# One layer of a hybrid decoder on one core: the first segment's output projection over all its tokens at once

## The chip, the core and the metric

The kernel runs on one core of one Trainium2 chip. The metric is the device time of one execution, in microseconds, as a median over runs. TensorE is written PE in the profile (PEld is its loading of stationary operands), VectorE is DVE, ScalarE ACT, GpSimd POOL and SyncE SP; SP issues nearly all DMAs here.

## What is computed

One layer over 2048 prompt tokens and 8 sample tokens, model width 1024, all in float32:

```python
h = _rmsnorm(x, norm_pre_mix)
(gq, gk, gv, gz, gb, ga, mq, mk, mv, mo, mi, mf) = _split(h @ w_in, IN_SPLITS)
...                                   # four heads of gated DeltaNet, four of mLSTM, by chunks
o = jnp.concatenate([o_gdn.reshape(Bsz, T, GDN_WIDTH), h_ml.reshape(Bsz, T, ML_WIDTH)], axis=-1)
mix = o.astype(h.dtype) @ w_out       # the output projection, 1024 x 1024
x = x + _rmsnorm(mix, norm_post_mix)
u = jnp.square(jax.nn.relu(_rmsnorm(x, norm_pre_mlp) @ w_up))
x = x + _rmsnorm(u @ w_down, norm_post_mlp)
```

## The kernel before

The prompt is cut into four segments of 512 tokens; the 8 sample tokens ride with the second one. Per segment there are stage A (input projection `w_a`, `a_units`), the recurrent mixer (`mixer`: two halves of gated DeltaNet, then four mLSTM chunks of 128 tokens, `ml_chunk`), stage B (output projection `w_o`, `b_units`), `norm_mid`, and the MLP (`cd_units`).

**A product.** Activations lie transposed, model width on partitions and tokens in columns. Every float32 operand is split into a rounded part and a rest, hi and lo, and three matmuls stand for one: hi by hi (L195), hi weights by lo activations (L196), lo weights by hi activations (L200). A `Half` is one 128x512 block of weights, that is four 128x128 tiles: one DMA of 256 KB into `wraw` (L171, four buffers), one ACT cast to hi (L178), one DVE subtraction to lo (L183), both into `whl` (three buffers), and 12 matmuls for each stretch of columns that it is given. A `unit` is two Halves, one for each half of the contracted width, and gives 128 output features in one PSUM bank `bk` (three buffers).

**Stage B of a segment.** The contracted width is 1024: the first half, `X0`, holds the four DeltaNet heads, the second, `X1`, the four mLSTM heads. The mixer's `out_T` transposes a chunk's result on PE (L702), multiplies it on DVE (L703) and writes it to DRAM, `dO` (L704). `b_prep` reads `dO` back into `xt` (two buffers; L1099), casts to hi on ACT (L1101) and subtracts to lo on DVE (L1102). It does so for tokens 0 to 255 and then for tokens 256 to 511 (`tok_halves`), each in four pieces of 128x(2x256). `b_units` makes 8 units for the first half of the tokens and the same 8 units again, weights loaded and split anew, for the second half. For each unit ACT copies the bank to `mixT` (L1110) and squares it (L1137, L1140), and POOL adds the square up (L1141). Between the two halves `ahead_norm` starts `norm_in` of segment 2, which loads rows of `x_prompt` (L285), squares them (L231), scales them (L233) and transposes them on PE (L244).

**Around it.** Ahead of stage B of segment 0 stand the last 16 Halves of stage A of segment 1, among which the last mLSTM chunks and the gate arithmetic of segment 1 are mixed: `gates` sums gate rows on PE (L390, L396), runs a series for log(1+exp) on DVE (L374 to L382, L411 to L413) and returns to PE (L416 to L424). For the sample tokens a small tile of gates goes to DRAM (`dgs`, L399) and is read back (`sg`, L830, L832), for ACT L846. Behind stage B stand `w_gate` and `w_a` of segment 2, with `norm_mid(0)` among them.

**What sets the order.** The program is written as one list (`main`) with generators mixed in, and a scheduler then sets each engine's order by priorities and by when it expects an operand to be there. Each engine runs its own list strictly in order, SP too: a DMA that waits keeps those behind it waiting.

Of the kernel before, what the change touches and what calls it, by code (L numbers as in the profile page):

```python
# [24 lines left out]
def program(tc, ctx, d, T):  # L25
# [14 lines left out]
    def sb(shape, tag, bufs=1, dt=F32):  # L40
        return wk.tile(shape, dt, tag=tag, name=tag, bufs=bufs)
# [95 lines left out]
    def width(s):  # L137
        return SEG + NB if s == SS else SEG

    def pieces(s):  # L140
        return [(0, 260), (260, 520)] if s == SS else [(0, 512)]
# [4 lines left out]
    def tok(s, tt):  # L146
        return (tt * 128, 128) if tt < 4 else (SEG, NB)

    def ctok(s, c):

        return s * SEG + (NB if s > SS else 0) + c
# [55 lines left out]
    def unit(src, acts, cols, done, packed=False):  # L207

        parts = [(None, c0, c1) for c0, c1 in cols]
        return [Half(src[:, i * 512:(i + 1) * 512], lambda i=i: acts()[i], parts, i == 0, i == 1, done, packed)  # L210
                for i in range(2)]
# [876 lines left out]
    def tok_halves(s):  # L1088
        return [(0, 256), (256, width(s))]

    def b_prep(s, halves):
        for c0, c1 in tok_halves(s):
            for g in range(2):
                for k0 in (0, 2):
                    t = sb([128, 1040], "xt", 2)
                    w = c1 - c0
                    tv = t[:, :2 * w].rearrange("p (a b) -> p a b", a=2)
                    kk = 4 * g + k0
                    Q.dma_start(tv, dO[s][kk:kk + 2, :, c0:c1].rearrange("j p t -> p j t"))  # L1099
                    hi, lo = (halves[g][:, k0:k0 + 2, i, c0:c1] for i in range(2))  # L1100
                    A.copy(hi, tv)  # L1101
                    V.tensor_tensor(lo, tv, hi.bitcast(F32), op=ALU.subtract)  # L1102
                    yield 1

    def b_units(s, halves, mixT, sums):
        out = []

        def evac(j, parts):
            for p, c0, c1 in parts:
                A.copy(mixT[0][:, j, c0:c1], p[:, :c1 - c0])  # L1110
                add_square(sums[0][:, 1], j, p[:, :c1 - c0], c0, c1)
        for cols in tok_halves(s):
            us = []
            for j in range(8):
                us += unit(d["w_o"][j], lambda: halves, [cols], lambda parts, j=j: evac(j, parts))
            out.append(us)
        return out

# [16 lines left out]
    def add_square(total, j, src, c0, c1):  # L1135
        if j == 0:
            A.activation(total[:, c0:c1], src, AF.Square, scale=1.0 / 32.0)  # L1137
        else:
            sq = tmp512()
            A.activation(sq[:, c0:c1], src, AF.Square, scale=1.0 / 32.0)  # L1140
            G.tensor_tensor(total[:, c0:c1], total[:, c0:c1], sq[:, c0:c1], op=ALU.add)  # L1141
# [30 lines left out]
    def tiles_of(s, c0, c1):  # L1172
        return [t for t in tts(s) if c0 <= tok(s, t)[0] < c1]

    def pairs(src, c0, c1, tag="xt"):

        w = c1 - c0
        k = 4 if 4 * w <= 1040 else 2

        def load(j):  # L1180
            t = sb([128, 1040], tag, 3 if tag == "xs" else 2)[:, :k * w].rearrange("p (a b) -> p a b", a=k)
            Q.dma_start(t, src[j:j + k, :, c0:c1].rearrange("j p t -> p j t"))
            return t
        ahead = load(0)
        for j in range(0, 8, k):
            t, ahead = ahead, load(j + k) if j + k < 8 else None
            yield j, k, t
# [3 lines left out]
    def norm_mid(s, mixT, halves, c0, c1, sums, pace):  # L1191

        mt, su = mixT[0], sums[0]
        tiles = tiles_of(s, c0, c1)
        o = ctok(s, 0)
        xs = pairs(d["xT"][:, :, o:o + width(s)], c0, c1)
        x = next(xs)
        r = sb([128, 5], "st", 4)
        yield pace[0]
        mean_square(s, [su[:, 1]], tiles, r, lambda out, p, i, n: V.tensor_scalar(out, p, EPS, None, op0=ALU.add))  # L1200
        for g in ([t for t in tiles if t < 4], [t for t in tiles if t == 4]):
            if g:
                n = tok(s, g[0])[1]
                rsqrt_to(r[:n, g[0]:g[-1] + 1], r[:n, g[0]:g[-1] + 1], 0.0)
        yield pace[0]
        spread(s, r, tiles, su[:, 3])
        yield pace[0]
        while x is not None:
            j0, k, xt = x
            x = next(xs, None)  # L1210
            for j in range(j0, j0 + k):
                y = tmp512()
                m = mt[:, j, c0:c1]
                V.scalar_tensor_tensor(y[:, c0:c1], m, gain[:, 1, j:j + 1], su[:, 3, c0:c1], op0=ALU.mult, op1=ALU.mult)  # L1214
                (G if j % 2 else V).tensor_tensor(m, y[:, c0:c1], xt[:, j - j0], op=ALU.add)
                hi, lo = (halves[j // 4][:, j % 4, i, c0:c1] for i in range(2))
                A.activation(hi, m, AF.Copy, scale=gain[:, 2, j:j + 1])
                V.scalar_tensor_tensor(lo, m, gain[:, 2, j:j + 1], hi.bitcast(F32), op0=ALU.mult, op1=ALU.subtract)  # L1218
                yield pace[1]
            Q.dma_start(dx1[s][j0:j0 + k, :, c0:c1].rearrange("j p t -> p j t"), mt[:, j0:j0 + k, c0:c1])  # L1220
        for j in range(8):
            add_square(su[:, 2], j, mt[:, j, c0:c1], c0, c1)
            yield pace[1] / 2


        if s not in e4s:
            e4s[s] = sb([128, 5], "e4", 2)
        e4 = e4s[s]

        def op(out, p, i, n):  # L1230
            V.tensor_scalar(out, p, EPS, None, op0=ALU.add)
            V.scalar_tensor_tensor(out, out, EPS, out, op0=ALU.mult, op1=ALU.mult)
        mean_square(s, [su[:, 2]], tiles, e4, op)
        yield 1
# [96 lines left out]
    main = []  # L1331
# [3 lines left out]
    def stream(gen, front=False):  # L1335
        if front:
            streams.insert(0, gen)
        else:
            streams.append(gen)
# [83 lines left out]
    def after(s):  # L1423

        oT, mixT, h2 = [], [], h2s[s]
        ahead = s + 2 if s < 2 and s + 2 < NSEG else None
        defer = s >= 2
        tail = tails.get(s - 1)
        hn, sums = [], sumss[s]
        before = sumss.get(s - 1)  # L1430
        w, wb = width(s), width(s - 1)

        def prep():
            flush()
            sums.append(row_sums())
            if before is not None:
                before[:] = sums
            h2[:] = act8("X")
            stream(b_prep(s, h2))

        def mix_tiles():
            mixT.append(sb([128, 8, SEG + NB], "Y0", 1) if defer else acc_t)

        def ahead_norm():
            if ahead is not None:
                hn[:] = act8("Y")
                stream(norm_in(ahead, hn))

        main.append(prep)
        if s == 0:  # L1450
            main.append(rate(1.0))
            main.extend(a1[-CUT:] if NSEG > 1 else [])
        main.extend(lasts.get(s - 1, []))
        if tail and not defer:
            main.extend(tail[0])
            main.append(lambda: stream(final(s - 1, 0, 256, before, FAST)))
            main.extend(tail[1])
            main.append(flush)
            main.append(lambda: stream(final(s - 1, 256, wb, before, FAST)))
        main.append(flush if s == 0 else (lambda: None))  # L1460
        main.append(mix_tiles)
        b = b_units(s, h2, mixT, sums)
        main.extend(b[0])
        if defer:
            main.append(lambda: stream(norm_mid(s, mixT, h2, 0, 256, sums, FAST)))
            main.extend(b[1])
            main.append(lambda: stream(norm_mid(s, mixT, h2, 256, w, sums, FAST)))
            for t in tail:
                main.extend(t)
            main.append(flush)  # L1470
            main.append(lambda: stream(final(s - 1, 0, wb, before, SLOW)))
        else:
            main.append(ahead_norm)
            main.extend(b[1])
            main.append(flush)
            main.append(lambda: stream(norm_mid(s, mixT, h2, 0, w, sums, SLOW)))
            if s == 0 and NSEG >= 3:
                main.append(lambda: stream(sample_mix(SS)))
            if ahead is not None:
                main.extend(a_units(ahead, hn, LIGHT))  # L1480
            main.append(flush)
# [109 lines left out]
```

## Time and profile before

| | us |
|---|---|
| median of three runs | 2653.05 |
| lowest and highest | 2652.44, 2653.79 |
| the profiled execution's own time | 2654.11 |
| its span in the trace | 2652.3 |

The page gives each engine's busy time and the chain of work that ended last. The trace behind it can be asked for each engine's instructions in order of time, for who waited for whom, and for busy time and granted TensorE clock by stretch. Matmuls are pipelined and their ends are modelled, so the time of a series of them is read from starts, not from durations.

### The profile page before, as it was taken

Reading aid. Unit: us, or ns where it says so; the run is one execution under the profiler, and the core shown is the slowest. Engines: PE = TensorE matmul, PEld = TensorE weight load, DVE = VectorE, ACT = ScalarE, POOL = GpSimd, SP = SyncE. Lnnn points to the kernel's source line nnn. Section 1 sums busy time; section 2 is a strip of 40 time slices with the busy share of each in tenths; the row PEclk is TensorE's granted clock in tenths of the full one; section 3 lists DMA queues with packets and bytes.
Section 4 is the critical chain, followed back from the end, with each engine's and each line's share of the span. In section 5 each row is a group of like instructions: output and inputs, shape, how many; then the busy total and the mean of one; then the engine's idle time right before and its main releaser. Section 6 shows DMA issues by size and latency. Waiting matters only on the chain.

```text
span 2652.3 us, 44344 instructions
## 1 busy us (share of the span) xinstructions
PE 2599.9 (98%) x15912; PEld 2268.5 (86%) x15912; DVE 1727.5 (65%) x3513; ACT 1283.5 (48%) x3120; POOL 433.3 (16%) x494
## 2 busy tenths in 40 slices
PE   8999999999999999999999999999999999999998
PEld 6879999787888788878899999997787888788887
DVE  7665758647747656774775766577758566765445
ACT  5636557435536345653655444466354355433332
POOL 2101112311000000530100000054000003552002
PEclk9999999999999999999999999999999999999999
DMA  5444457654324345754433343455333346565222
GB/s 173 155 147 144 151 152 222 207 156 134 108 92 126 96 141 167 236 186 135 139 97 110 107 141 119 138 173 163 99 112 112 106 144 205 182 197 147 93 96 84
DMA packets 292221, 377.40 MB, mean 142 GB/s; under 512 B 42325, under 2 KB 147785, under 8 KB 291993
## 3 DMA queue, kind: packets, MB, share of 16 engines
q1 hardware_dynamic: 289312, 365.13, 44.2%
q0 software_dynamic: 2688, 9.44, 1.3%
q8 instruction: 126, 2.06, 0.3%
q14 instruction: 95, 0.77, 0.1%
HBM read 314.04 MB, written 60.53 MB: 141 GB/s over the span
## 4 chain that ended last, share of the span: by engine, by line
PE 88%; DVE 4%; DMA 4%; issue 2%; ACT 1%; POOL 0%; SPq 0%; DVEq 0%; ACTq 0%; POOLq 0%
PE bk L195 26%; PE bk L196 26%; PE bk L200 26%; DMA wraw<-w_o 1%; DVE whl L183 1%; DVE nt L1214 1%; DMA xt<-x_prompt 1%; DVE X L1218 1%; DMA xt<-dO 1%; PE mx L563 1%; PE mx L655 1%; PE mx L770 1%; PE mx L680 1%; PE mx L681 1%; PE mx L747 1%
## 5 line engine op out<-in xcount | busy, mean ns | idle before, releaser
L178 ACT CAST whl<-wraw 128x512 fp32r<-128x512 f32 x872 | 539.4, 620 | 933.7 <-PE bk L200 866.3
L183 DVE TENSOR_TENSOR whl<-wraw,whl 128x512 fp32r<-128x512 f32 (+1 forms) x872 | 636.3, 732 | 447.5 <-ACT whl L178 433.3
L195 PE MATMUL bk<-Y,whl 128*128 128x512 f32 (+2 forms) x2208 | 733.9, 347 | 4.2 <-ACT whl L178 2.0
L196 PE MATMUL bk<-Y,whl 128*128 128x512 f32 (+2 forms) x2208 | 732.1, 346 | 0.0
L195 PE MATMUL bk<-X,whl 128*128 128x512 f32 (+3 forms) x2024 | 654.9, 340 | 7.2 <-ACT whl L178 7.1
L196 PE MATMUL bk<-X,whl 128*128 128x512 f32 (+3 forms) x2024 | 653.5, 339 | 2.7 <-DVE X L1218 2.5
L200 PE MATMUL bk<-Y,whl 128*128 128x512 f32 (+2 forms) x2176 | 488.2, 344 | 6.9 <-DVE whl L183 6.9
L195 PEld LDWEIGHTS bk<-Y,whl 128*128 128x128 f32 x2208 | 416.2, 189 | 58.9 <-ACT whl L178 3.4
L196 PEld LDWEIGHTS bk<-Y,whl 128*128 128x128 f32 x2208 | 416.9, 189 | 50.4
L200 PE MATMUL bk<-X,whl 128*128 128x512 f32 (+3 forms) x2024 | 442.4, 339 | 8.9 <-DVE whl L183 8.8
L195 PEld LDWEIGHTS bk<-X,whl 128*128 128x128 f32 x2024 | 381.8, 189 | 50.5 <-ACT whl L178 9.5
L196 PEld LDWEIGHTS bk<-X,whl 128*128 128x128 f32 x2024 | 381.7, 189 | 47.5 <-DVE X L1218 4.1
L200 PEld LDWEIGHTS bk<-Y,whl 128*128 128x128 f32 x2176 | 359.1, 189 | 59.5 <-DVE whl L183 8.6
L200 PEld LDWEIGHTS bk<-X,whl 128*128 128x128 f32 x2024 | 326.3, 188 | 54.3 <-DVE whl L183 11.5
L1262 DVE TENSOR_TENSOR acc<-acc,bk 128x512 f32<-128x512 f32 (+2 forms) x296 | 164.3, 557 | 157.3 <-PE bk L200 153.4
L1141 POOL TENSOR_TENSOR NQ<-NQ,nt 128x256 f32<-128x256 f32 (+4 forms) x145 | 143.3, 991 | 470.5 <-ACT nt L1140 464.1
L1251 DVE TENSOR_TENSOR tB<-tB 128x512 f32<-128x512 f32 (+1 forms) x160 | 96.9, 608 | 44.1 <-ACT Y L1250 43.1
L305 DVE SCALAR_TENSOR_TENSOR tB<-tA,cw,tB 128x512 f32<-128x512 f32 x144 | 108.0, 750 | 13.6 <-ACT tB L301 9.3
L1252 DVE TENSOR_TENSOR Y<-tB,Y 128x512 fp32r<-128x512 f32 (+1 forms) x160 | 98.0, 615 | 3.2
L596 DVE TENSOR_TENSOR W<-xt 32x30 f32<-32x30 f32 (+14 forms) x240 | 76.2, 317 | 22.3 <-DMA xt<-dn 17.5
L1249 ACT ACTIVATE tB<-bk 128x512 f32<-128x512 f32 (+1 forms) x160 | 81.8, 511 | 16.1 <-PE bk L200 13.0
L1250 ACT ACTIVATE Y<-tB 128x512 fp32r<-128x512 f32 (+1 forms) x160 | 87.2, 549 | 4.3
(397 smaller groups left out, 2481.8 us busy)
## 6 DMA issues: line engine op xcount, KB each, us to landing
wraw<-w_dn SPq DMA_DIRECT2D x264, 256.0 KB, 2.8
wraw<-w_up SPq DMA_DIRECT2D x256, 256.0 KB, 2.8
wraw<-w_a SPq DMA_DIRECT2D x224, 256.0 KB, 2.9
wraw<-w_o SPq DMA_DIRECT2D x128, 256.0 KB, 3.3
dqkv<-tB SPq DMA_DIRECT2D x48, 256.0 KB, 3.3
gb<-drb SPq DMA_DIRECT2D x32, 256.0 KB, 3.8
qk<-dqkv SPq DMA_DIRECT2D x16, 512.0 KB, 5.7
dzo<-tB SPq DMA_DIRECT2D x32, 256.0 KB, 3.3
```

The source lines that it names most:

```text
L178: A.copy(self.hl[:, 0], self.raw)
L183: V.tensor_tensor(lo, raw, hi.bitcast(F32), op=ALU.subtract)
L195: PE.matmul(o, lhsT=w, rhs=acts[:, k, 0, c0:c1], start=(self.first and k == 0), stop=False)
L196: PE.matmul(o, lhsT=w, rhs=acts[:, k, 1, c0:c1], start=False, stop=(self.packed and self.last and k == 3))
L200: PE.matmul(o, lhsT=w, rhs=acts[:, k, 0, c0:c1], start=False, stop=(self.last and k == 3))
L305: V.scalar_tensor_tensor(acc, pre[:, t:t + SEG], cw[:, j, t:t + 1], acc, op0=ALU.mult, op1=ALU.add)
L1141: G.tensor_tensor(total[:, c0:c1], total[:, c0:c1], sq[:, c0:c1], op=ALU.add)
L1249: A.activation(r[:, :n], p[:, :n], AF.Relu)
L1250: A.activation(sl[:, 0, c0:c1], r[:, :n], AF.Square)
L1251: V.tensor_tensor(r[:, :n], r[:, :n], r[:, :n], op=ALU.mult)
L1252: V.tensor_tensor(sl[:, 1, c0:c1], r[:, :n], sl[:, 0, c0:c1].bitcast(F32), op=ALU.subtract)
L1262: V.tensor_tensor(a, a, p[:, :c1 - c0], op=ALU.add)
```

## The change

For segment 0 alone (512 tokens, no sample tokens) stage B takes all columns in one pass: `b_cols` returns one stretch of 512 columns in place of two of 256. `b_prep` then works in four pieces of 128x(2x512), of which the two for `X1` need all four mLSTM chunks. `b_units` makes 8 units of two Halves, 16 Halves in place of 32. `ahead_norm` is put after the first 4 of the 8 units. Segments 1 to 3 keep their order.

```diff
+    def b_cols(s):
+        return [pieces(s)] if s == 0 else [[h] for h in tok_halves(s)]
+
     def b_prep(s, halves):
-        for c0, c1 in tok_halves(s):
+        for cols in b_cols(s):
+            c0, c1 = cols[0][0], cols[-1][1]
...
-        for cols in tok_halves(s):
+        for cols in b_cols(s):
             us = []
             for j in range(8):
-                us += unit(d["w_o"][j], lambda: halves, [cols], lambda parts, j=j: evac(j, parts))
+                us += unit(d["w_o"][j], lambda: halves, cols, lambda parts, j=j: evac(j, parts))
...
-        main.extend(b[0])
         if defer:
+            main.extend(b[0])
...
         else:
+            b = sum(b, [])
+            main.extend(b[:len(b) // 2])
             main.append(ahead_norm)
-            main.extend(b[1])
+            main.extend(b[len(b) // 2:])
```

New lines move the code behind them by 5 lines from the second loop of `b_prep` on: L1099 becomes L1104, L1101 becomes L1106, L1102 becomes L1107, L1110 becomes L1115.

TensorE, where the last mLSTM chunk's result is transposed (`mx<-ident,on`, L702). `X0_4529` and `X1_4530` are the two halves of the contracted width, `whl_` a Half's split weights, `bk_` a unit's bank. Before:

```order
L200 MATMUL bk_5233<-X0_4529,whl_5207 128x256
L702 MATMUL mx_3791<-ident_68,on_3729 128x128
L390 MATMUL mx_3798<-pairsum_74,grow_2414 128x16
...
L702 MATMUL mx_3791<-ident_68,on_3729 128x128 x2
L390 MATMUL mx_3798<-pairsum_74,grow_2414 128x16 x2
L396 MATMUL mx_3805<-grow_2414,pairsum_74 16x8
L200 MATMUL bk_5233<-X0_4529,whl_5207 128x256 x3
L195 MATMUL bk_5233<-X1_4530,whl_5228 128x256
```

And now:

```order
L702 MATMUL mx_3791<-ident_68,on_3729 128x128
L390 MATMUL mx_3798<-pairsum_74,grow_2414 128x16 x4
L396 MATMUL mx_3805<-grow_2414,pairsum_74 16x8
...
L200 MATMUL bk_5178<-X0_4529,whl_5152 128x512 x2
L702 MATMUL mx_3791<-ident_68,on_3729 128x128 x2
...
L416 MATMUL mx_3903<-gl_3846,triu_70 128x32
L417 MATMUL mx_3903<-gl_3846,ones_66 128x32
L423 MATMUL mx_3908<-ident_68,gl_3846 4x128
...
L195 MATMUL bk_5102<-X1_4530,whl_5097 128x512
L195 MATMUL bk_5139<-X1_4530,whl_5134 128x512
L195 MATMUL bk_5178<-X1_4530,whl_5173 128x512
```

Before, the chunk's transposes are followed by seven more Halves for tokens 0 to 255 and by one Half over `X0` for the others, ahead of the first matmul on `X1` of tokens 256 to 511. Now only two matmuls on `X0` and the gates' ten stand between the last transpose and the first matmul on `X1`; three Halves over `X0` have run by then (banks 5102, 5139 and 5178), and all three banks wait for `X1`.

SyncE, from the last chunk's write to `dO` on. Before:

```order
L704 DMA dO0_141<-on_3789 128x4x128
L399 DMA dgs_154<-t16_3807 16x8
L171 DMA wraw_5270<-w_o 128x512
L1099 DMA xt_4771<-dO0_141 128x2x256
L1099 DMA xt_4806<-dO0_141 128x2x256
L171 DMA wraw_5288<-w_o 128x512
L830 DMA sg4_6467<-dgs_154 128x4x32
L832 DMA sg4_6467<-dgs_154 32x1
```

And now:

```order
L399 DMA dgs_154<-t16_3807 16x8
L830 DMA sg4_6141<-dgs_154 128x4x32
L704 DMA dO0_141<-on_3789 128x4x128
L832 DMA sg4_6141<-dgs_154 32x1
L171 DMA wraw_5176<-w_o 128x512
L832 DMA sg4_6141<-dgs_154 32x1
L1104 DMA xt_4614<-dO0_141 128x2x512
L1104 DMA xt_4649<-dO0_141 128x2x512
```

The read-back of the sample gates (L830, which has to wait for L399 to land) now stands ahead of the last chunk's write to `dO`, and the reads of `dO` are twice as large.

## Rows read from the trace of the kernel before

**Rows 1.** The page's first part: the span, then busy time, share and instructions of TensorE.

```profile
span 2652.3 us, 44344 instructions
PE 2599.9 (98%) x15912; PEld 2268.5 (86%) x15912; DVE 1727.5 (65%) x3513; ACT 1283.5 (48%) x3120; POOL 433.3 (16%) x494
```

**Rows 2.** TensorE's waits, 400 to 475 us: engine line, releaser: total us, times, longest.

```profile
PE bk L195 <- ACT whl L178: 1.5, 2, 1.0
```

**Rows 3.** Timeline, TensorE in stage B: start us, us, engine line op; first matmuls of two Halves.

```profile
428.53 0.28 PE L195 MATMUL bk<-X,whl 128*128 128x256 f32 x1
...
429.94 0.28 PE L195 MATMUL bk<-X,whl 128*128 128x256 f32 x1
```

**Rows 4.** Timeline, TensorE in stage A of segment 2: first matmuls of two Halves.

```profile
535.90 0.40 PE L195 MATMUL bk<-Y,whl 128*128 128x512 f32 x1
...
538.70 0.39 PE L195 MATMUL bk<-Y,whl 128*128 128x512 f32 x1
```

**Rows 5.** The chain that ended last, 405 to 475 us: start us, us, what.

```profile
418.44 0.22 PE mx L747 x2
...
426.29 0.53 DVE on L703
...
427.07 2.92 DMA dO<-on
430.00 3.44 DMA xt<-dO
433.47 0.63 ACT X L1101
434.12 0.70 DVE X L1102
434.84 4.48 DMA xt<-x_prompt
```

**Rows 6.** Timeline, ScalarE, 409 to 446 us; in brackets the idle time before and its end.

```profile
422.69 1.15 ACT L764 ACTIVATE on<-mx,fac 128x128 f32<-128x128 f32 x4
...
436.91 0.23 ACT L846 ACTIVATE sbeta<-sg 128x33 f32<-128x33 f32 x1 [1.51 <-DMA sg<-dgs]
...
439.35 1.06 ACT L231 ACTIVATE xs<-xt 128x1024 f32<-128x1024 f32 x1 [0.33 <-DMA xt<-x_prompt]
```

**Rows 7.** Timeline, VectorE, the same stretch.

```profile
427.09 0.14 DVE L398 COPY t<-mx 16x8 f32<-16x8 f32 x1
...
441.75 1.23 DVE L233 TENSOR_SCALAR xs<-xt,st 128x1024 f32<-128x1024 f32 x1
```

**Rows 8.** Timeline, SyncE's queue, the same stretch: when a DMA was issued.

```profile
427.50 0.49 SPq L399 DMA_DIRECT2D dgs<-t  x1
...
431.50 0.38 SPq L830 DMA_DIRECT2D sg<-dgs  x1
431.93 0.49 SPq L832 DMA_DIRECT2D sg<-dgs  x1
```

**Rows 9.** Timeline, TensorE: the first of the gates' ten matmuls, and the matmul behind them.

```profile
441.11 0.30 PE L416 MATMUL mx<-gl,triu 128*128 128x32 f32 x2
...
442.27 0.37 PE L195 MATMUL bk<-X,whl 128*128 128x256 f32 x1
```

**Rows 10.** TensorE at 497 to 512 us: waits, two matmuls, and the stretch with its granted clock (PEclk).

```profile
PE bk L200 <- DVE whl L183: 3.6, 2, 2.6
...
509.65 0.63 PE L195 MATMUL bk<-Y,whl 128*128 128x512 f32 x1
510.08 0.63 PE L196 MATMUL bk<-Y,whl 128*128 128x512 f32 x1
...
core 0: us, PE busy (x) PEld busy (x) DVE busy (x) ACT busy (x) POOL busy (x), PEclk, DMA share, GB/s
500.00:550.00 50.00, 45.85 (x208) 36.20 (x207) 29.15 (x50) 19.78 (x34) 22.00 (x9) 0.97 0.58 183
```

**Rows 11.** DMA issues: out<-in, engine, op, count, KB each, median us to landing.

```profile
qk<-dqkv SPq DMA_DIRECT2D x16, 512.0 KB, 5.7
...
dn<-NQ SPq DMA_DIRECT2D x32, 32.0 KB, 1.7
```

## The prediction

> **What bounds the kernel now.** I read the page's first part: TensorE is busy 98% of a span of 2652.3 us [rows 1]. So an edit pays only by shortening TensorE's own list or by taking waits out of it, and costs what it puts in as waits. Then I compared the two orders of each engine. They differ between the second half of segment 0's mixer and `norm_mid(0)`; from about 530 us on they are the same, so the whole effect has to come from there. TensorE's waits around stage B show what can be won: 1.5 us, two waits for a cast of weights [rows 2]. Last I followed the chain that ended last through the stage, since it holds, duration by duration, the path from the last mLSTM chunk to stage B's operand [rows 5].
>
> **TensorE's own work.** Twelve matmuls of 256 columns take 1.41 us from the first start of one Half to that of the next [rows 3], twelve of 512 columns 2.80 us [rows 4]. Stage B is 32 Halves before, 45.1 us, and 16 after, 44.8 us: 0.3 us won. Half as many matmuls and weight loads are nearly worth nothing, because the time goes by columns, and these stay.
>
> **Removed splits.** 16 DMAs, 16 casts and 16 subtractions go. They lay beside the matmuls on engines with room, so they count only where TensorE waited for them: the 1.5 us of [rows 2]. I take all of it off; were it to come back in another place, it is 0.
>
> **The new wait.** This is the large term. Before, tokens 0 to 255 needed only two mLSTM chunks, and Halves of these tokens covered the last chunk's way out. Now every matmul on `X1` needs the last chunk. I count from the end of that chunk's last product, 418.66 us, the start and length of L747 in [rows 5], and call it zero.
>
> The way out, by durations of before: normalisation up to the last L764 takes until 423.84, that is +5.2 [rows 6]. TensorE needs 19 matmuls on `X0`, 4.4 us at 0.233, up to its first transpose L702, so it gets there before the operand does, and L702 starts at about +5.3. Four transposes, the gates' sums and four matmuls on `X0` later, at about +6.8, L703 starts; before, it was +7.6 (426.29). It takes 0.53 us, so the chunk is ready to be written at +7.4.
>
> But in SP's new order the write L704 stands behind L830, and L830 waits until L399 has landed. L399 follows L398, which before came 0.8 us after L703's start [rows 5, 7] and is now placed ahead of it: L399 goes out at about +6.8. No row shows how long it takes to land. The smallest transfer with a landing took 1.7 us [rows 11], and L830 was issued 4.0 us after L399, where other things stood between [rows 8]; so L830 goes out at +8.5 to +10.8 and L704, 0.4 us later, at +8.9 to +11.2. I take the middle, +10.0, for no row is nearer.
>
> The write takes 2.92 us, to +12.9. The read was 3.44 us for 256 KB; it is 512 KB now, for which the row next in the same chain has 4.48 us, and 5.7 us is the median of loads that go out in pairs as these do [rows 5, 11]. I take 4.48, +17.4, since its queue was loaded with the same neighbours. The cast of 1024 columns takes 1.06 us where that of 512 took 0.63 [rows 5, 6]. `X1` can be used at **+18.5**. By the low ends (no hold by L830, write at +8.0, a read of 3.44) it is +15.5, by the high ends (+11.2, 5.7) +20.9.
>
> The gates ahead of it on TensorE come at the same time: L846 had its input 5.0 us after the first L832 was issued [rows 6, 8], so at about +15.4 now; L847 and eight short DVE steps behind it, estimated at 0.2 us each from L398's 0.14 and the like, bring L416 to about +17.3, and the ten matmuls take 1.16 us [rows 9]. They don't release TensorE sooner than `X1` does.
>
> TensorE has only 23 matmuls on `X0` to do until then, 5.4 us, and four transposes and the gates' sums, about 1.2 us. So it waits **11.9 us** (0.9 of them for L764), in which the gates' 1.16 us, run elsewhere before, find room: 10.7 net, between 7.7 and 13.1.
>
> **What is queued behind it.** All of TensorE's list, `w_gate` of segment 2 included. Of SP's: the loads of `x_prompt` for segment 2 wait for the two `xt` buffers that the reads of `dO` hold. They start some 4 us later than before and have 20 us of matmuls as cover: nothing. The lo part of `X1` (a subtraction of 1.23 us [rows 7] behind the gates' copy) is wanted after the first three matmuls, 0.7 us: 0.5 us more. The split of the next weights waits for one of three `whl` buffers, all held by `X1` Halves: 0.2 us more, as the three banks end staggered.
>
> **The clock.** After TensorE's longest wait in this neighbourhood, 2.6 us, matmuls of 512 columns started 0.43 us apart for a while, which is its 1.2 GHz level, and the stretch of 50 us had a mean granted clock of 0.97 [rows 10]. That is 3 us at half, 1.5 us lost. A wait four times as long should do the same at least once: 1.5 us, from 0 (if the fall lies wholly inside the wait) to 3.
>
> **Sum.** -0.3 - 1.5 + 10.7 + 0.7 + 1.5 = **+11.1 us**. The profiled execution took 2654.11 us, 1.06 above the median of three; against it the sum gives 2665.2, against the median 2664.2. I predict **2664 us**. By all low ends it is -0.3 - 1.5 + 7.7 = +5.9, by all high ends -0.3 + 13.1 + 0.7 + 3 = +16.5.
>
> **A page beside it.** The Trainium skill, DMA: Bandwidth & Descriptors (Anatomy of one DMA), fits a transfer, for the GpSimd path, with 2.0 us plus its bytes over 436 GB/s. By it the write of 256 KB would take 2.6 us and the read of 512 KB 3.2 us; this trace has 2.92 and 4.48 on SP's path [rows 5], and the measurement decides. By the page the sum would be 1.6 us less, 2662.6. The same page (Rules for kernel authors) advises to issue a DMA early and to wait for it late, which speaks against this change, and so does the trace.
>
> **Rivals.** *The norm gets lighter (no change).* Behind stage B, at 497 to 509 us, TensorE waited 3.6 us for DVE's splits, which stood behind `norm_mid`'s steps, and fell to 1.2 GHz for it, 1.5 us: 5.1 us in all [rows 10]. In the new order of DVE the splits stand one or two places earlier among these steps. If that frees them all, +11.1 becomes +6.0, and with the wait at its low end, 3 us less, +3.0: 2656. For it: the order. Against: POOL and DVE have the same work there. *The way out is covered (faster).* Should the scheduler's expectation hold, that three Halves over `X0` suffice, there is no wait at all, and -0.3 - 1.5 - 5.1 = -6.9: 2646. It decides at a way out of 7 us; before it took 16.2 (418.66 to 434.82, the end of L1102), of which the write and the read alone are 6.4 [rows 5]. *The queue holds longer (slower still).* L830 holds the write by 4 us or more, the pair of reads takes 5.7 us, the clock falls twice: +16.5, 2669.5. For it: the order on SP. *The change does nothing* is excluded, the list has 16 Halves of 512 columns.
>
> **How the numbers follow.** Forecast 0.70; slower still 0.11; lighter norm 0.13; covered 0.06. The range takes the forecast's bounds and the lighter norm's time: 2656 to 2669; what lies outside is the covered way and the ends of two others, under 2 in 10. Within 0.2% (5.3 us, about what a measurement of this kernel tells from no change) lie most of the lighter norm's cases: 0.12. Slower: 0.82. Faster: 0.06.
>
> **What would show it.** In the profile after: a gap on TensorE of some 11 us, the gates' ten matmuls within it, between the last L200 on `X0` and the first L195 on `X1`, ended by the cast L1106, by L416 or by both, with SP's L830 ahead of L704; half-spaced starts behind it; stage B's first matmul to `w_gate` longer by some 10 us; Halves 2.8 us apart. I am wrong if the write goes out less than 1 us after L703, if `X1` is cast within 10 us of the last L747, or if the waits at 497 to 509 us are gone.

## The result

| | us |
|---|---|
| kernel before, median of 4 runs | 2652.74 (2651.41 to 2653.79) |
| changed kernel, median of 4 runs | 2668.85 (2663.78 to 2671.01) |
| ratio | 1.0052, 95% interval 1.004 to 1.0064 |
| profiled execution of the changed kernel | 2668.06, span 2666.4 |

The change makes the kernel slower by about half a per cent. A later measurement of the same two texts, on another occasion, gave 1.0036 (1.0023 to 1.005).

The first part of the page, against [rows 1]: TensorE executes 192 instructions fewer and is busy 2.8 us longer, in a span 14.1 us longer.

```profile
span 2666.4 us, 43813 instructions
PE 2602.7 (98%) x15720; PEld 2261.2 (85%) x15720; DVE 1725.5 (65%) x3493; ACT 1274.5 (48%) x3084; POOL 426.2 (16%) x487
```

TensorE's waits of after, 400 to 490 us (engine line, releaser: total us, times, longest), against [rows 2]:

```profile
PE mx L416 <- DVE gl L412: 7.7, 1, 7.7
PE bk L195 <- ACT whl L178: 0.7, 1, 0.7
```

The 1.5 us of waits for weight casts have become 0.7, and a wait of 7.7 us has come in. It does not end at the operand `X1`, as one might look for it, but at the gates of segment 1 (L416). The timeline of TensorE around it (start us, us, engine line op; idle time before and its end in brackets):

```profile
422.03 0.39 PE L747 MATMUL mx<-v,E 128*128 128x130 f32 x2
...
429.55 0.71 PE L200 MATMUL bk<-X,whl 128*128 128x512 f32 x2
437.95 0.61 PE L416 MATMUL mx<-gl,triu 128*128 128x32 f32 x2 [7.69 <-DVE gl L412]
...
440.27 0.42 PE L424 MATMUL mx<-ident,gt 128*4 128x128 f32 x1
440.34 1.63 PE L195 MATMUL bk<-X,whl 128*128 128x512 f32 x3
...
442.19 0.63 PE L195 MATMUL bk<-X,whl 128*128 128x512 f32 x1
442.62 1.05 PE L196 MATMUL bk<-X,whl 128*128 128x512 f32 x2
...
444.51 0.39 PE L195 MATMUL bk<-X,whl 128*128 128x512 f32 x1
444.74 0.40 PE L196 MATMUL bk<-X,whl 128*128 128x512 f32 x1
```

The last L747 ends at 422.42 (zero below). The last matmul on `X0` starts at +7.4 and the first on `X1` at +17.9. Behind the gates' group matmuls of 512 columns start 0.43 us apart, which is the 1.2 GHz level (the granted clock of 433.95 to 444.19 us is 0.50); from 444.51 on they are 0.23 apart again. ScalarE, and SyncE's queue in the same place:

```profile
435.72 0.23 ACT L846 ACTIVATE sbeta<-sg 128x33 f32<-128x33 f32 x1 [4.80 <-DMA sg<-dgs]
439.03 1.04 ACT L1106 CAST X<-xt 128x1024 fp32r<-128x1024 f32 x1 [3.08 <-DMA xt<-dO]
```

```profile
429.07 0.32 SPq L399 DMA_DIRECT2D dgs<-t  x1
430.38 0.37 SPq L830 DMA_DIRECT2D sg<-dgs  x1
431.16 0.37 SPq L704 DMA_DIRECT2D dO<-on  x1
431.59 0.49 SPq L832 DMA_DIRECT2D sg<-dgs  x1
...
435.52 0.88 SPq L1104 DMA_DIRECT2D xt<-dO  x2
```

The cast that makes `X1` usable ends at 440.07, 0.27 us before the first matmul on it. So two chains end together: the gates' small tile through DRAM (L399, L830, L846, L847, L412, L416), and the last chunk through DRAM (L704, L1104, L1106). Which of them costs the time, the trace alone does not tell.

### The profile page after: what moved, and what is told of

Its sections match the earlier page's. It is cut to its first block, busy times and chain, and to the rows that moved or that the text cites. A ratio compares the mean times of both kernels' runs of the same rounds, so it can differ in the third digit from the quotient of the medians.

```text
span 2666.4 us, 43813 instructions
## 1 busy us (share of the span) xinstructions
PE 2602.7 (98%) x15720; PEld 2261.2 (85%) x15720; DVE 1725.5 (65%) x3493; ACT 1274.5 (48%) x3084; POOL 426.2 (16%) x487
## 4 chain that ended last, share of the span: by engine, by line
PE 88%; DVE 4%; DMA 4%; ACT 2%; issue 1%; POOL 0%; SPq 0%; DVEq 0%; ACTq 0%; POOLq 0%
PE bk L195 26%; PE bk L196 26%; PE bk L200 26%; DVE whl L183 1%; DMA xt<-x_prompt 1%; DVE X L1223 1%; DVE nt L1219 1%; DMA wraw<-w_o 1%; PE mx L563 1%; DMA xt<-dO 1%; PE mx L655 1%; PE mx L681 1%; PE mx L680 1%; PE mx L672 1%; PE mx L663 1%
## 5 line engine op out<-in xcount | busy, mean ns | idle before, releaser
L178 ACT CAST whl<-wraw 128x512 fp32r<-128x512 f32 x856 | 529.1, 620 | 939.7 <-PE bk L200 879.0
L183 DVE TENSOR_TENSOR whl<-wraw,whl 128x512 fp32r<-128x512 f32 (+1 forms) x856 | 626.9, 735 | 452.4 <-ACT whl L178 441.5
L195 PEld LDWEIGHTS bk<-X,whl 128*128 128x128 f32 x1960 | 370.8, 189 | 54.2 <-ACT whl L178 10.5
L196 PEld LDWEIGHTS bk<-X,whl 128*128 128x128 f32 x1960 | 370.8, 189 | 50.4 <-DVE X L1223 4.1
L200 PEld LDWEIGHTS bk<-X,whl 128*128 128x128 f32 x1960 | 321.3, 189 | 58.0 <-DVE whl L183 12.5
```

The lines of the kernel that those rows point to most:

```text
L178: A.copy(self.hl[:, 0], self.raw)
L183: V.tensor_tensor(lo, raw, hi.bitcast(F32), op=ALU.subtract)
L195: PE.matmul(o, lhsT=w, rhs=acts[:, k, 0, c0:c1], start=(self.first and k == 0), stop=False)
L196: PE.matmul(o, lhsT=w, rhs=acts[:, k, 1, c0:c1], start=False, stop=(self.packed and self.last and k == 3))
L200: PE.matmul(o, lhsT=w, rhs=acts[:, k, 0, c0:c1], start=False, stop=(self.last and k == 3))
```

## Experiments

The stage can be measured in each trace without the spread of whole runs. TensorE's list holds one group of `w_gate` matmuls for each segment; that of segment 1 stands ahead of the stage and that of segment 2 behind it. In before their first rows are these; the difference, 274.65 us, is called **the stretch**:

```profile
196.16 0.29 PE L195 MATMUL bk<-Y,whl 128*128 128x260 f32 x1
...
470.81 0.39 PE L195 MATMUL bk<-Y,whl 128*128 128x512 f32 x1
```

And in after, 284.50 us:

```profile
198.27 0.29 PE L195 MATMUL bk<-Y,whl 128*128 128x260 f32 x1
...
482.77 0.40 PE L195 MATMUL bk<-Y,whl 128*128 128x512 f32 x1
```

All kernels, one trace each; "stage" runs from the end of segment 0's last L747 to the second group (the expectations have 60.5 us for it in after, with a border 0.2 us earlier):

| kernel | stretch | of it the stage | time to before, 95% interval |
|---|---|---|---|
| before | 274.65 | 52.15 | |
| before again | 274.68 | 52.17 | 0.9998 (0.9987 to 1.0009) |
| after | 284.50 | 60.35 | 1.0052 (1.004 to 1.0064) |
| after again | 284.16 | 60.13 | 1.0036 (1.0023 to 1.005) |
| `X1` from another tensor | 274.02 | another order | 1.0001 (0.9993 to 1.001) |
| filler in the hole | 284.90 | 60.51 | 1.0047 (1.0032 to 1.0062) |
| gates later | 282.91 | 59.56 | 1.0042 (1.0029 to 1.0055) |
| two reads, wide units | 281.69 | 59.52 | 1.0017 (1.0008 to 1.0026) |
| one read, narrow units | 290.16 | 67.77 | 1.0056 (1.0042 to 1.007) |
| both: gates later, two reads | 282.41 | 58.45 | 1.0025 (1.0013 to 1.0038) |
| half the units in token halves | 274.60 | 51.75 | 1.0006 (0.9996 to 1.0016) |
| before, gates later | 278.03 | 56.02 | 1.0014 (1.0004 to 1.0023) |

Theory T: all of `X1` must make the round trip of the last chunk through DRAM, and three `X0` Halves are all that can run meanwhile. Rival R: the sample gates' read-back, which the scheduler put ahead of L704 and of L416, is the cause. Rival W: 512-wide Halves, reads and casts cost by themselves.

### The same kernels again

Edit: none.

> The changed kernel once more, unedited, on a chip of its own, so that its traces can be laid beside each other. Between the two profiled runs of before and after, 8.4 us of the difference lie between the end of the last L747 of segment 0 and the first w_gate matmul of segment 2 (52.15 us before, 60.52 after); some 5.6 us lie in stretches whose instructions the change does not touch: 2.1 at a half-clock stretch at 31.2 to 34.6 us, 1.4 between 250 and 410 us, 2 between 1095 and 1188 us. Theory A (these 5.6 us are the draw of that one execution): ratio of medians between 1.003 and 1.0055, and in the new trace the 31 us stretch is at full clock or the 1095 to 1188 us stretch has before's length. Theory B (they follow from the change, by what lies later in time): ratio again 1.005, and both stretches are as long as in the first trace of after.

> The kernel before once more, unedited, for a second trace of it. If the stage lengths are the program's own: 274.65 us between the two w_gate halves again, within 1 us, and a ratio of 1.000 within 0.0015. If they are draws of one execution: other by 2 us or more.

The stretch repeats to 0.03 us in before and 0.34 in after, so the +9.7 us is the program's own. What lies outside it is mostly the draw of an execution: the time ahead of the first group was 196.2 and 199.8 us in the two traces of before, 198.3 and 196.5 in those of after. At 31.2 to 34.6 us the granted clock was 0.50 in after's first trace and 1.00 in its second, and before's second trace has a half-clock stretch there too, with PEclk 0.99 over 195 us where its first had 1.00:

```profile
0.00:195.00 195.00, 181.72 (x890) 148.27 (x891) 131.97 (x302) 107.17 (x244) 24.02 (x54) 0.99 0.49 157
```

Theory A holds for these pieces but not for all of them: the 1.4 us ahead of stage B, counted among the draws, came again. From the first group to the last L747 it took 222.50 and 222.51 us in before, 224.15 and 224.03 in after. That came with the change, and was not in the sum.

### The wait taken away

```diff
-                    Q.dma_start(tv, dO[s][kk:kk + 2, :, c0:c1].rearrange("j p t -> p j t"))
+                    src = dzo if s == 0 and g == 1 else dO
+                    Q.dma_start(tv, src[s][kk:kk + 2, :, c0:c1].rearrange("j p t -> p j t"))
```

> The changed kernel, but X1 of segment 0 (the second four rows of k) is read from dzo[0], which is written long before, in place of dO[0]; same sizes and number of DMAs, casts and matmuls, and the output of the first segment is therefore not the reference's. Nothing of the output projection waits for the last chunk of the mixer any more. Theory T (the whole loss of stage B is the round trip of the last chunk through dO): L747 to w_gate falls from 60.5 to 50 to 52 us, no wait over 1 us ahead of X1, no half clock there; the time is 8 to 11 us below the changed kernel, 2652 to 2660, and what stays above before, if anything, is the part that lies outside stage B. Rival W (512-wide halves, larger reads and casts cost by themselves): stage B stays above 56 us.

TensorE's waits, 400 to 490 us, and the stretch's busy time (PE, PEld, DVE, ACT, POOL), PEclk, DMA share, GB/s:

```profile
PE bk L195 <- ACT Y L249: 0.5, 1, 0.5
```

```profile
410.00:490.00 80.00, 79.44 (x419) 66.12 (x418) 54.69 (x144) 44.96 (x122) 19.38 (x14) 1.00 0.44 118
```

Neither the hole nor the half clock is left in this window; the stretch is 274.02 us, 0.6 below before, and the time is that of before. The scheduler also moved `X1` Halves ahead of the mixer's end, so the stage by itself can't be compared, and this run changes the order together with the operand. It does show that what the change costs is gone when `X1` is there early, and W falls. It also hints at the ceiling: with 0.5 us of waits left here, wide Halves and 16 removed splits are worth 0.6 us of a trace and nothing that the runs can tell (ahead of the last L747 TensorE waited 3.1 us, 1.3 more than in before).

### Work put into the hole

```diff
                 o = p[:, :c1 - c0]
+                for _ in range(self.rep - 1):        # rep = 3 for the third unit's X0 Half
+                    for k in range(12):
+                        PE.matmul(o, lhsT=self.hl[:, k // 8, k % 4 * 128:(k % 4 + 1) * 128], rhs=acts[:, k % 4, 0, c0:c1], start=(k == 0), stop=(k == 11))
```

> The changed kernel with 24 matmuls of 512 columns added, 5.6 us of TensorE work whose result the group's first real matmul overwrites, directly behind the third unit's X0 half and ahead of L416; every other instruction keeps its place. Theory T (TensorE stands idle for 7.7 us since X1 of all tokens is late, so what stands in that hole is free): the idle time ahead of L416 falls from 7.7 to about 2.1 us, L416 starts at the same 15.7 us after the last L747, and the half-clock stretch of 434.0 to 444.2 us shrinks or goes, so the time is 0 to 3.1 us below the changed kernel's. Rival W (the kernel is slow because of TensorE's own wide halves, and the hole is only where their time shows): 5.6 us slower than the changed kernel.

```profile
PE mx L421 <- DVE gl L417: 2.3, 1, 2.3
PE bk L200 <- ACT X L1111: 1.2, 1, 1.2
...
```

(Lines are shifted by 5: L421 is L416, L1111 is L1106.) 5.6 us of additional TensorE work cost 0.4 to 0.7 us of stretch, and the gates' group starts 15.7 us after the last L747, 15.5 in after. So the hole is set by the chains. With the idle time cut, the mean granted clock at 410 to 490 us is 0.98 (the second line), where after (the first) had 0.94:

```profile
410.00:490.00 80.00, 71.61 (x367) 59.22 (x366) 47.04 (x132) 42.37 (x109) 13.62 (x13) 0.94 0.47 140
```

```profile
410.00:490.00 80.00, 75.76 (x395) 62.64 (x394) 47.73 (x136) 43.02 (x112) 13.88 (x13) 0.98 0.47 139
```

The clock still fell once, to 0.50 at 441.6 to 445.0 us. And this brought no time back: the write L704 went out at +9.6 in place of +8.7 and `X1` came at +18.4, so what the group gained at full clock went into 1.2 us of waiting for the cast. That part of the expectation failed.

### The gates' round trip taken out

```diff
-            gs = sb([128, 16], "t16", 2)
+            gs = const([128, 16], "gkeep")
...
-            Q.dma_start(dgs[:, :].rearrange("k (h b) -> (k h) b", h=4), gs[:16, :NB])
+            later["gs"] = gs          # written to dgs and read back in sample_mix, behind its convolution
```

> The changed kernel with the write and read-back of the sample gates (L399, L830, L832 and the L846, L847 behind them) taken out of the queues at the end of segment 0 and done in the sample's own stage. Theory T (X1 of all tokens is what is late): L704 issues up to 0.8 us earlier and the two X1 casts follow, L416's group runs in the hole's shadow, X1 begins 0.5 to 1.5 us earlier: 0.5 to 3 us below the changed kernel. Rival R (the read-back of the gates, 4.04 us, that stands ahead of L416 on VectorE is the cause): the 7.7 us go, and with them the half clock: 8 to 11 us below, at the time of before.

The chain that ended last, in this kernel (start us, us, what), with the last L747 ending at 420.75:

```profile
428.15 0.75 DVE on L703
428.93 2.39 DMA dO<-on
431.33 4.52 DMA xt<-dO
435.87 1.05 ACT X L1109
```

```profile
PE mx L416 <- DVE gl L412: 4.5, 1, 4.5
PE bk L195 <- ACT X L1109: 1.1, 1, 1.1
...
```

Now the chain runs over `dO`, as T says. L704 goes out at +8.2 in place of +8.7, and the write lands 2.4 us later, where in after 4.4 us passed between L704 and L1104 with the reads of `sg` in the same queue. The wait falls by 2.0 us, to two pieces of 5.7 together, and the stretch by 1.3 to 1.6, of which 0.7 to 0.9 are shorter waits ahead of the last L747; R, which asked for 8 to 11, falls. In the whole time nothing of it can be told.

The control, the same edit on the kernel before:

> The kernel before with the sample gates' write and read-back moved to the sample's stage, as a control. Theory T: before has sixteen halves whose operands are there while the round trip runs, so it gains nothing: 274.65 us between the w_gate halves within 0.6, ratio 1.000 within 0.0015. Rival R (the gates' DMAs cost by themselves wherever they stand): 1.2 us or more less.

It gains nothing in time, as T has it (it is rather slower: 1.0014, and the interval leaves out 1), but its stretch is 278.03 us, out of the expected range. The next one, from the second `w_gate` group to the third, is shorter by as much: 941.9 us for both together, against 941.1 and 943.1 in the two traces of before. The order around the second group changed with the edit (and the clock fell to 0.50 at 466.2 to 469.6 us, some 9 us ahead of the group), so for this kernel the stretch is not a fair measure.

### Width and read apart

Two reads of 256 columns, units 512 wide:

```diff
-        for cols in b_cols(s):
-            c0, c1 = cols[0][0], cols[-1][1]
+        for c0, c1 in tok_halves(s):          # in b_prep alone
```

> The changed kernel with b_prep reading dO[0] in two pieces of 256 columns again, units still 512 wide. Theory T: the X0 cover ahead of the wait is the same three halves of 2.80 us, so most of the wait stays; X1 comes up to 1.4 us earlier (shorter read, cast of 0.63 in place of 1.04), but L416 stands ahead of it at 15.7 us after the last L747 as before: 0 to 1.5 us below the changed kernel, 282.7 to 284.5 us between the two w_gate halves. Rival P (the one-pass read of 512 columns is the loss): back at before, 274 to 276 us.

One read of 512 columns, all 32 Halves as before (the edit is made on the kernel before):

```diff
-        for c0, c1 in tok_halves(s):
+        for c0, c1 in (pieces(s) if s == 0 else tok_halves(s)):     # in b_prep alone
```

> The kernel before with only the read of dO[0] in one pass of 512 columns (the other half of the edit, units of 512 columns, is left out): all 32 halves of 256 columns stay, but X1 is late for all of them. Theory T (X1 of all tokens comes some 18 us after the last L747, and only as many X0 halves as there are bk banks lie ahead of it): the three X0 halves ahead are 1.41 us each in place of 2.80, 4.2 us less, so the wait ahead of L416 and X1 grows from 7.7 to about 12 us and what is left to do behind it is 4.2 us more; from the w_gate half at 196 us to that at 470 us it takes 287 to 289.5 us (274.65 in before, 284.2 and 284.5 in the two traces of after); 3 to 5 us above the changed kernel. Rival W (the width of the units is what costs): between before and the changed kernel.

With two reads the wait is still there:

```profile
PE mx L416 <- DVE gl L412: 6.3, 1, 6.3
...
```

The stretch is 2.5 to 2.8 us shorter, below the 282.7 to 284.5 expected, and far above P's 274 to 276: P falls, but the narrow reads are worth more than T allowed. The stage alone, 0.6 to 0.8 us shorter, understates it. Ahead of the last L747 (222.17 us from the first group) TensorE's order is that of before again, and three `X0` matmuls of 512 columns and four L770, some 1.15 us of work, stand behind that border and not ahead of it as in after. Some 0.5 us of the gain are shorter waits ahead of the border, and the other 2 us are the stage's: TensorE waited 6.6 us in it, where after had 8.4 and 8.3.

With one read the narrow units lose most, 15.5 us of stretch against before:

```profile
PE mx L416 <- DVE gl L412: 8.6, 1, 8.6
PE bk L195 <- ACT whl L178: 2.8, 2, 2.1
...
```

Less of `X0` lies ahead of the wait, three Halves of 1.41 us in place of 2.80, and 4.2 us more of matmuls are left behind it. That was T's direction and sign. The wait itself did not grow to about 12 us as T had it, but to 8.6, since L416 came at +13.7 in place of +15.5. The amount, 5.7 to 6.0 us over after, is above the 3 to 5 expected, 2.1 us of it in a wait for a weight cast. So the loss does not come with the width: the narrow units lose more, and what matters is how much work that needs nothing of the last chunk stands ahead.

Both edits on the changed kernel, gates later and two reads:

> Both edits together on the changed kernel: the sample gates' write and read-back moved to the sample's stage, and dO[0] read in two pieces of 256 columns. Alone the two took the stretch between the w_gate halves from 284.2 and 284.5 us to 282.9 and 281.7. Theory T (X1 and the gates' group arrive within half a microsecond of each other in the changed kernel, so that taking one away shows little of it): together more than the larger of the two, 279.5 to 281 us, and a wait of 3 to 5 us left ahead of X1, which is the round trip itself; the time 3 to 5 us below the changed kernel and still above before. Rival G (the two are one and the same gain): 281.5 us or more.

```profile
PE bk L195 <- ACT X L1108: 6.2, 1, 6.2
...
```

The gates are behind `X1` now, and the one long wait left ends at the cast of `X1`. By its figure T missed: 282.41 us is 1.4 above its range and lies where G was to be. The part ahead of the stage holds 3.0 us of waiting for a load of the mixer at L578, which the other kernels had at 0.3 to 1.4. With TensorE's waits ahead of the last L747 taken off, the stretch is 281.6 and 281.3 us in the two traces of after, 280.8 with the gates later, 279.4 with two reads and 278.3 with both. So the two edits are not the same gain, against G, but together they give 3.0 to 3.2 us, hardly more than the sum of what each gives alone, 0.5 to 0.7 and 2.0 to 2.2. That each hides the other, as T had it, is not shown. The wait left, 6.2 us, is more than the 3 to 5 expected, since L704 was no earlier than in after (+8.7).

### The cover given back

Units 0 to 3 in token halves, as before, units 4 to 7 wide; the change's read is undone.

```diff
...
-            b = sum(b, [])
-            main.extend(b[:len(b) // 2])
+            b = [b[0][:8] + b[1][:8], b[2]]      # first halves of units 0-3, second halves, then wide units 4-7 (s == 0)
+            main.extend(b[0])
             main.append(ahead_norm)
-            main.extend(b[len(b) // 2:])
+            main.extend(b[1])
```

> Units 0 to 3 of the first segment in token halves as before (first halves of all four, then second halves), units 4 to 7 over all 512 tokens, read in two pieces: the early units' first token halves need nothing of the last chunk, so 8 halves of 1.41 us and three more X0 halves, 15.5 us of work, lie ahead of the first X1 half that must wait, in place of 8.4. Theory T: the wait falls under 1.5 us, no half clock behind it, 273.5 to 276 us between the two w_gate halves; the time is that of before within 0.1%. Rival W (512-wide halves cost by themselves): 278 us or more.

```profile
PE bk L195 <- ACT whl L178: 1.5, 2, 0.8
PE bk L195 <- ACT X L1106: 0.3, 1, 0.3
```

```profile
410.00:490.00 80.00, 78.14 (x500) 69.19 (x499) 55.28 (x149) 49.37 (x128) 17.36 (x17) 1.00 0.62 181
```

The wait for `X1` is 0.3 us, the clock is full, the stretch 274.60. The whole loss is gone with half of the units still wide; the time can't be told from before's. Two reads with all units wide took 281.69: what lies between is the work that the narrow first units put ahead of the wait. T stands. A version that beats both did not appear, and `X1` from another tensor shows why there was little to look for here.

## Why the prediction was right, and where it was not

It said +11.1 us and 2664; the runs gave 2668.85, within the range, and the stretch +9.7. The mechanism was right, a wait of TensorE for the last chunk's way through DRAM, and the size by parts that were off in both directions. Some of it is luck: the range ends 0.15 us above the measured time, and the medians differ by 16.1 us in the first measurement and by 10.9 in the later one, where the changed kernel's 2669.37 lies outside the range. By its own steps, with the waits and the busy share of TensorE in the stage:

```profile
418.66:470.81 52.15, 50.45 (x431) 49.50 (x430) 43.28 (x126) 39.57 (x109) 14.99 (x18) 1.00 0.74 225
```

```profile
422.42:482.77 60.35, 51.95 (x244) 41.61 (x244) 36.67 (x110) 31.82 (x80) 11.73 (x11) 0.92 0.48 143
```

The first line is before, the second after. Idle time grew from 1.7 us (52.15 less 50.45) to 8.4, busy time by 1.5: +8.2.

- **TensorE's own work** and **removed splits**: as predicted. The waits for weights of before, 1.5 and 0.2 us, are gone from this stage; 16 wide Halves save 0.2 us. Busy time at full clock shrank by more than that, by some 1.6 us (1.5 less 3.1 of clock, below): four L770 and four L1153 matmuls, estimated at 0.1 us each, lie inside before's window and outside after's, which makes 0.8 (the L770 turn up again in the last point); 0.6 us of it I can't place.
- **The new wait**: right as a mechanism, 1.1 us too large. The idle times, 7.7 and 0.7, and the gates' group, 2.4 at half clock, make a hole of 10.8 us, against 11.9. Less 1.16 for the group it is 9.6 net, against 10.7. Four steps of the way were off, and mostly balanced. The chunk was ready to be written at +8.2, not +7.4 (L703 started at 429.83 and took 0.75 us). The hold of L704 by L830 was shorter: L399 landed in 1.3 us, so L704 went out at +8.7 and not at +10.0, 0.6 us after L703's end. But the write then took 4.4 us until the read could be issued, not 2.92: the reads of `sg` ran in the same queue (2.39 in the kernel without them). The read took 3.5 us until the cast, not 4.48. The cast and the subtraction, which the prediction priced by L231 and L233, other operations on as many columns, took 1.04 and 1.23 us as it said. `X1` was there at +17.7, predicted +18.5; L416 at +15.5, predicted +17.3.
- **"They don't release TensorE sooner than X1 does"**: this held within 0.3 us, but the two chains swapped places. The wait ended at L416, and the group behind it, slowed by the clock, filled the time until `X1`.
- **What covered the wait before**: nine Halves of tokens 0 to 255 (first matmuls from 427.12 to 439.70) and one over `X0` (442.27) stand in before between the last transposes and the first `X1` matmul of tokens 256 to 511 (443.77), not seven and one.
- **What is queued behind it**: 0.7 us were expected at the weights and the rest of `X1`. The 0.7 found, at a weight cast, stands ahead of the hole and is counted in it.
- **The clock**: it fell as said, once, for longer than assumed. From L416 at 437.95 to some 444.2 (the first start at full pace is at 444.51) TensorE worked at 1.2 GHz: 3.1 us of working time, of which 1.2 in the gates' group (2.4 less 1.16, counted in the hole) and 1.9 on `X1`, against 1.5 predicted.
- **Not in the sum**: 1.5 to 1.65 us ahead of the last L747. The prediction saw that the orders differ from the second half of the mixer on, but gave that part no term. 0.45 us of it are the four L770: in before they start at 418.50, behind that border, in after ahead of it, so for the stretch they are no loss. The rest is waiting: 2.9 and 2.8 us from the first group to the last L747 in the two traces of after, 1.8 in both of before. TensorE's waits there, before and then after:

```profile
PE bk L195 <- ACT whl L178: 1.4, 1, 1.4
PE mx L578 <- ACT junk L531: 0.4, 1, 0.4
```

```profile
PE bk L195 <- ACT whl L178: 1.6, 2, 0.8
PE mx L578 <- ACT junk L531: 1.3, 1, 1.3
```

So 1.0 to 1.2 us of waits are what the sum lacked. Without its waits that part repeats: 220.7 us in both traces of before, 221.2 in both of after, 219.9 in both kernels with two reads and all units wide. Why L578 and the weight casts wait longer in after stays open; no kernel was made to tell.

So +8.2 for the stage (predicted +11.1: wait -1.1, clock +0.4, no 0.7 behind it, and some 1.4 of own work that went elsewhere or that I can't place), +1.5 ahead of it, and the rest of the first comparison's 16 us, with that much of spread among whole runs, I take for what two sets of four runs drew; with the later set, medians 2669.37 and 2658.47, it is 10.9.

**The rivals.** *The norm gets lighter* came in a small part. TensorE's waits at 490 to 570 us, after and then before:

```profile
PE bk L200 <- DVE whl L183: 4.6, 3, 2.0
```

```profile
PE bk L200 <- DVE whl L183: 3.6, 2, 2.6
PE bk L195 <- ACT whl L178: 0.5, 1, 0.5
```

They are no less in total, 4.6 against 4.1 us, only in shorter pieces. But the half-clock stretch of [rows 10], priced at 1.5 us of that rival's 5.1, is not there in the two traces of after (PEclk 1.00 at 500 to 550 us), and both traces of before have it (0.97 and 0.93). *The way out is covered* fell with the 7.7 us. *The queue holds longer* was wrong in its place: it was not the hold that grew, but the write behind it. Of the prediction's own signs of being wrong none came, though one is a matter of reading: the write went out 1.3 us after the start of L703, but only 0.6 after its end.

## What to carry to other kernels

Joining two halves of a stage joins their operands: the first of the joined work waits for the last operand of both. Count what can run without the last operand, against the operand's whole way (here 5.4 us of `X0` matmuls, left when the last product ended, against 17.7), before counting saved instructions. It was enough here to keep the first four of eight units in halves; wide and narrow matmuls took nearly the same time for the same columns (2.80 us against twice 1.41).

## What the runs showed of the hardware

The sample gates' reads, one of 64 KB ahead of the 256 KB write and four of 0.1 KB behind it, go with a slow write. From the issue of L704 to that of the read of `dO` it took 4.1 to 4.4 us in the five traces with these reads next to it, and 2.4 to 3.0 in five kernels where they come later or not at all (2.39 in both with wide units and the gates later). Their own tile landed 4.04 us after the first small one was issued (the chain that ended last in after):

```profile
431.59 4.04 DMA sg<-dgs
```

The Trainium skill, DMA: Bandwidth & Descriptors (Rules for kernel authors), says that transfers under 64 KB pay mostly overhead, and (Issuing engines are not separate DMA queues) that DMAs run on the same 16 engines and interleave. The trace agrees with the first by these 4.04 us; the 2.0 us that the write took beyond 2.39 fit the second, though with the gates' reads other things moved too.

After an idle time of 7.7 us TensorE was at 1.2 GHz with its first matmul behind the gap, and stayed there for some 6 us of work; with 5.6 us of that gap filled, the mean granted clock at 410 to 490 us went from 0.94 to 0.98.

Ahead of the first `w_gate` group, where TensorE's list is the same in all of these kernels, one execution took 196.2 us and another 201.1. The stretch between two fixed instructions, which repeated within 0.4 us, told apart what the medians could not.
